# A decoder trunk on one core: the last MLP's down products with two groups in the seven-product form, and low weight parts made by adding transfers

## The chip, the cores and the metric

The kernel runs on one core of a Trainium2 chip. The metric is the device time of one execution in microseconds. Before the change the median of three runs is 2835.14 us (2832.22 to 2835.55). The execution that was profiled took 2834.88 us; the span from its first to its last profiled instruction is 2832.0 us.

## The reference, cut to what matters

Two decoder layers work on x (256 tokens by 2048 features, float32). Each layer is a token mixer, an attention over a memory of 256 rows, and a squared-ReLU MLP, each behind an RMS norm and added to x; a last RMS norm follows.

```python
def squared_relu_mlp(h, w_up, w_down):
    return jnp.square(jax.nn.relu(h @ w_up)) @ w_down      # w_up 2048 x 8192, w_down 8192 x 2048

for i in range(DEPTH):                                     # DEPTH = 2
    ...                                                    # mixer, then memory attention with x_w_o at its end
    x = x + squared_relu_mlp(rms_norm(x, g_ff[i]), f_w_up[i], f_w_down[i])
return rms_norm(x, g_final)
```

The change touches the down product of the second layer's MLP and, in the order of its steps, the output product (x_w_o) of both attentions.

## The kernel before, in words

**Float32 by three products.** TensorE multiplies in a rounded float32 format (fp32r). Each operand is split into a high part (its rounded copy) and a low part (operand minus high part), and a product is high times high, high times low and low times high. `split` (L100) makes both parts: ScalarE (ACT) casts `hi`, VectorE (DVE) subtracts `lo = src - hi`.

**Weights** come as tiles of 128x1024 float32 (512 KB, two k tiles of 128 rows by 512 columns): `wload` (L115) lets SyncE (SP) load one into `wraw` (4 buffers), and `wtile` splits it into `whi` and `wlo` (3 buffers each). A direct product with one weight tile has 12 matmuls of 512 columns: 2 k tiles, 2 halves of the tokens, 3 parts.

**The last MLP** (`mlp`, `nxt.closing`) goes in four blocks `b` of 2048 hidden features. A block first makes its hidden features with 8 calls of `gemm_feat` (32 weight tiles; here called the up stage): ACT and DVE evacuate each result, square it and split it into `hh` and `hl`. Then it multiplies with 16 k tiles of `w_down` by 4 column chunks of 512 (the down stage). Two column chunks together are a pair. Seven pairs go through `gemm_seven`: two in each of the blocks 0 to 2 and one in block 3. The last two column chunks go through `gemm_hid` and `gemm_last`.

**The seven-product form.** Take 4 k tiles as two halves, the tokens as two halves and the two column chunks. The direct product of these 2x2x2 blocks is 8 block products of 6 matmuls. With sums of the token side (`token_sums`, made once a block) and differences of the weights it is 7 block products, some of which go into two results: 42 matmuls in place of 48. The differences are `raw - raw` on DVE, 128x1024 each, and each of the 7 weight operands is then split on its own. Products are called P1 to P7 here after the steps of the new code. Before the change 4 of the 16 k tiles take this form and 12 are direct, so a pair has 42 + 144 = 186 matmuls, 19 splits and 4 differences. Two small results (`kept`) are copied out by ACT and added into x by DVE (`gather`, L617); at the end of a pair four more `gather`s read the accumulators, two as soon as the first half of the last direct products is done and two at the very end.

**Order.** The program is written against tiles; a scheduler puts the instructions of each engine into a fixed order and sets the semaphores. Each engine then works through its own list in order, and an instruction that waits holds up all behind it.

## Time and profile before

| | |
|---|---|
| median of three runs | 2835.14 us |
| profiled execution, time and span | 2834.88 us, 2832.0 us |
| TensorE (PE) busy | 2798.7 us (99%) |
| DVE, ACT, POOL busy | 1958.4, 1393.7, 200.3 us |
| last MLP, block 0: up stage, pair 1, pair 2 | about 90.4, 42.4 and 43.8 us |
| DMA | 579.55 MB, mean 205 GB/s |

Durations of matmuls in the profile overlap: one of 512 columns lasts 0.39 us, but the next starts about 0.23 us after it. How long a stage takes is read from starts, not from the sum of durations. DVE and ACT instructions that follow each other without a wait overlap by nearly 0.1 us.

### The profile page before, as it was taken

What the parts mean: (1) busy time and instruction counts of PE and PEld (TensorE: products, weight loads), DVE (VectorE), ACT (ScalarE), POOL (GpSimd) and SP (SyncE); (2) the same over time, 40 slices, a digit from 0 to 9 for tenths busy, and PEclk for the clock granted to TensorE, in tenths of its full rate; (3) what the DMA queues carried; (4) which work ended last, traced back from release to release, by engine and by line L of the source; (5) the groups of instructions that cost most, each with busy time, mean ns of one, the idle gap of its engine ahead of it and who ended that gap; (6) DMA issues with size and microseconds to landing.
All of it is one profiled execution on the core that took longest, in us unless ns stands there. A gap on an engine that the chain in (4) does not pass through costs nothing.

```text
span 2832.0 us, 39687 instructions
## 1 busy us (share of the span) xinstructions
PE 2798.7 (99%) x15172; PEld 2346.5 (83%) x15172; DVE 1958.4 (69%) x2707; ACT 1393.7 (49%) x1801; POOL 200.3 (7%) x374
## 2 busy tenths in 40 slices
PE   9999999999999999999999999999999999999998
PEld 7888888888888888888777788888888888888886
DVE  6855655578878788787567666556676767667665
ACT  5545544454544444444455445444454545445453
POOL 0100000001022222222011000000000000000000
PEclk9999999999999999999999999999999999999999
DMA  8766665657677777777879766566556576575755
GB/s 287 238 199 204 193 180 186 180 156 237 195 220 215 224 223 220 217 223 211 236 249 286 217 213 200 175 187 192 171 179 217 163 223 186 170 217 163 221 160 155
DMA packets 180847, 579.55 MB, mean 205 GB/s; under 512 B 37440, under 2 KB 39664, under 8 KB 179888
## 3 DMA queue, kind: packets, MB, share of 16 engines
q1 hardware_dynamic: 142304, 513.34, 59.0%
q0 software_dynamic: 38208, 63.62, 8.3%
q8 instruction: 118, 1.93, 0.3%
q14 instruction: 73, 0.60, 0.1%
q10 hardware_dynamic: 144, 0.07, 0.0%
HBM read 553.88 MB, written 22.94 MB: 204 GB/s over the span
## 4 chain that ended last, share of the span: by engine, by line
PE 88%; DVE 4%; DMA 4%; issue 2%; ACT 1%; POOL 0%; DVEq 0%; POOLq 0%; SPq 0%; ACTq 0%
PE acc L166 23%; PE acc L149 21%; PE acc L681 14%; PE acc L168 12%; PE acc L766 4%; PE acc L765 4%; PE acc L764 4%; DVE wlo L102 2%; DMA Kd<-kd 1%; PE ps L547 1%; PE ps L490 1%; DMA wraw<-in_f_w_down 1%; PE ps L149 1%; ACT whi L101 1%; PE ps L217 1%
## 5 line engine op out<-in xcount | busy, mean ns | idle before, releaser
L102 DVE TENSOR_TENSOR wlo<-wraw,whi 128x1024 fp32r<-128x1024 f32 x908 | 1108.5, 1222 | 660.8 <-ACT whi L101 656.8
L101 ACT CAST whi<-wraw 128x1024 fp32r<-128x1024 f32 x908 | 955.0, 1052 | 1128.6 <-PE acc L166 360.3
L166 PE MATMUL acc<-act,whi 128*128 128x512 f32 x3072 | 1082.9, 396 | 0.9 <-ACT whi L101 0.8
L168 PE MATMUL acc<-act,wlo 128*128 128x256 f32 x3072 | 865.0, 282 | 1.7 <-DVE wlo L102 1.5
L166 PEld LDWEIGHTS acc<-act,whi 128*128 128x128 f32 x3072 | 576.0, 188 | 133.9 <-ACT whi L101 1.7
L149 PE MATMUL acc<-whi,act 128*128 128x512 f32 x1984 | 623.5, 393 | 8.6 <-ACT whi L101 6.9
L168 PEld LDWEIGHTS acc<-act,wlo 128*128 128x128 f32 x3072 | 580.4, 189 | 7.0 <-DVE wlo L102 3.4
L149 PEld LDWEIGHTS acc<-whi,act 128*128 128x128 f32 x1984 | 373.0, 189 | 86.6 <-ACT whi L101 6.9
L149 PE MATMUL acc<-wlo,act 128*128 128x512 f32 x992 | 387.7, 391 | 2.0 <-DVE wlo L102 2.0
L149 PEld LDWEIGHTS acc<-wlo,act 128*128 128x128 f32 x992 | 187.0, 189 | 40.5 <-DVE wlo L102 2.9
L765 PE MATMUL acc<-wlo,hh 128*128 128x512 f32 x544 | 215.1, 395 | 0.2 <-DVE wlo L102 0.2
L764 PE MATMUL acc<-whi,hh 128*128 128x512 f32 x544 | 214.5, 394 | 0.0
L766 PE MATMUL acc<-whi,hl 128*128 128x512 f32 x544 | 214.4, 394 | 0.0
L681 PE MATMUL acc<-wlo,hh 128*128 128x512 f32 x378 | 147.6, 390 | 1.7 <-DVE wlo L102 1.6
L681 PE MATMUL acc<-whi,hh 128*128 128x512 f32 x378 | 147.6, 390 | 0.5
L681 PE MATMUL acc<-whi,hl 128*128 128x512 f32 x378 | 147.2, 389 | 0.0
L681 PE MATMUL acc<-whi,act 128*128 128x512 f32 x432 | 135.8, 389 | 0.0
L765 PEld LDWEIGHTS acc<-wlo,hh 128*128 128x128 f32 x544 | 102.2, 188 | 24.4 <-DVE wlo L102 1.5
L766 PEld LDWEIGHTS acc<-whi,hl 128*128 128x128 f32 x544 | 102.2, 188 | 22.8 <-issue 1.6
L764 PEld LDWEIGHTS acc<-whi,hh 128*128 128x128 f32 x544 | 102.2, 188 | 22.2 <-issue 0.4
L681 PEld LDWEIGHTS acc<-whi,act 128*128 128x128 f32 x432 | 80.8, 188 | 16.7 <-ACT kept L710 0.2
L681 PEld LDWEIGHTS acc<-wlo,hh 128*128 128x128 f32 x378 | 71.0, 188 | 17.9 <-DVE wlo L102 3.1
(320 smaller groups left out, 2562.5 us busy)
## 6 DMA issues: line engine op xcount, KB each, us to landing
wraw<-in_f_w_up SPq DMA_DIRECT2D x256, 512.0 KB, 4.2
wraw<-in_f_w_down SPq DMA_DIRECT2D x228, 512.0 KB, 4.3
wraw<-in_a_w_in SPq DMA_DIRECT2D x64, 512.0 KB, 4.5
wraw<-in_x_w_q SPq DMA_DIRECT2D x64, 512.0 KB, 3.7
wraw<-in_x_w_k SPq DMA_DIRECT2D x64, 512.0 KB, 3.7
wraw<-in_x_w_v SPq DMA_DIRECT2D x64, 512.0 KB, 3.7
wraw<-in_b_w_out SPq DMA_DIRECT2D x64, 512.0 KB, 4.4
wraw<-in_x_w_o SPq DMA_DIRECT2D x48, 512.0 KB, 3.9
```

Of the source, the lines that this page charges most:

```text
L101: self.nc.scalar.copy(out=hi, in_=src)
L102: self.nc.vector.tensor_tensor(out=lo, in0=src, in1=hi.bitcast(F32), op=ALU.subtract)
L149: nc.tensor.matmul(out[t], pairs[m][0][:, kt, sl], pairs[m][1][:, kk, :], start=st and m == 0, stop=en and m == 2)
L166: nc.tensor.matmul(acc[:, f, :], hi[:, kk, sl], both[:, kt].rearrange("p a s -> p (a s)"), start=st, stop=False, skip_group_check=True)
L168: nc.tensor.matmul(acc[:, f, 0:S], lo[:, kk, sl], ah[:, kt, :], start=False, stop=en, skip_group_check=True)
L217: nc.tensor.transpose(pt[:, kk, t * P:(t + 1) * P], src[:, t, c:c + P], self.ident)
L490: mm = lambda s, m, b, e: nc.tensor.matmul(sc[:, t, :], s, m, start=b, stop=e, skip_group_check=True)
L547: mm = lambda s, mv, b, e: nc.tensor.matmul(op[:, k, :], s, mv, start=b, stop=e, skip_group_check=True)
L681: mm = lambda s, m, e: nc.tensor.matmul(out, s, m, start=key not in begun, stop=e, skip_group_check=True)
L764: nc.tensor.matmul(acc[:, t, :], ah[:, kt % 4, sl], hi[:, kk, :], start=st, stop=False)
L765: nc.tensor.matmul(acc[:, t, :], ah[:, kt % 4, sl], lo[:, kk, :], start=False, stop=False)
L766: nc.tensor.matmul(acc[:, t, :], al[:, kt % 4, sl], hi[:, kk, :], start=False, stop=en)
```

## The change

`gemm_seven` becomes `gemm_pair`, which takes its steps from a list of words. In the last MLP a pair now has **two groups** in the seven-product form (8 of 16 k tiles), and each numbered step makes its product for both groups. `d0`, `d1` are direct weight tiles of column chunk 0 or 1; `l0`, `l1` are direct tiles whose parts were **made ahead**: ACT casts the high part out of `wraw` into a home in `room`, a second ACT instruction writes minus the high part into another home, and a transfer that POOL issues reads the same 512 KB of weights from memory once more and adds them to it. `room` has homes for two such tiles at a time, so the parts for the tile after the next are begun when a tile's matmuls are emitted. Two tiles are begun before the MLP. `room` also holds the token sums. It takes one of the two buffers of `act`, which the attention's output features have held until then.

The weights of the seven-product form now have 8 buffers (`ws`, 4 before), the running difference `run` is gone (differences are made in place), and the results of `gemm_feat` share the buffers of `kept`. In both attentions one group is left, but the list now starts with P1 and then P5; before it was P5, P1.

Counted in the built programs, the last MLP loses 42 matmuls (14532 to 14490 in all). On DVE 14 splits of 128x1024 fall away, 28 differences of 128x1024 and one more `token_sums` a block (four additions of 128x256 and a split) come in. ACT has 14 casts fewer and, for the 35 made tiles, 70 instructions of 128x1024 more, beside 4 casts for sums. POOL issues 35 transfers of 512 KB more.

```diff
+ONE_GROUP = "1 5 2 d1 6 d1 7 d0 4 d1 3 d0 d1 d0 d1 d0 d0".split()
+TWO_GROUPS = "1 5 2 l1 6 l1 7 l1 4 l0 3 l0 d0".split()
...
-            ws = lambda: mp.tile([P, KB * NB], F32, name="ws", bufs=4)
-            sm = lambda: mp.tile([P, 4, 2, P], F32R, name="sums", bufs=2)
-            run = lambda: mp.tile([P, KB * NB], F32, name="run", bufs=1)
-            kept = lambda i: mp.tile([P, NB], F32, name="kept", bufs=4)
+            ws = lambda: mp.tile([P, KB * NB], F32, name="ws", bufs=8)
+            kept = lambda i=None: mp.tile([P, NB], F32, name="kept", bufs=4 if nxt.closing else 2)
+            if nxt.closing:
+                room = self.act.tile([P, 8, KB * NB], F32R, name="room", tag="act")
+                homes = cycle(range(4))
...
+                low = self.low_parts(lambda: room[:, next(homes)], made)
+                for _ in range(2):
+                    low[1]()
...
-                    if nxt.closing and n == 0:
-                        sums = self.token_sums(ws(), sm, *rs)
+                    if nxt.closing and n < 2:
+                        sh, sl = (room[:, 4 + 2 * n + i].rearrange("p (s k c) -> p s k c", s=4, k=2) for i in range(2))
+                        sums.append(self.token_sums(ws(), iter((sh, sl)).__next__, *rs))
...
+        def more():
+            for w, n, kc in islice(plan, 1):
+                hi, lo = home(), home()
+                nc.scalar.copy(out=hi, in_=self.wload(w, n, kc))
+                nc.scalar.activation(out=lo, in_=hi.bitcast(F32), func=AF.Copy, scale=-1.0)
+                nc.gpsimd.dma_start(out=half(lo), in_=w[n, kc], accum_op=ALU.add)
+                ready.append((half(hi), half(lo)))
...
+        def block(key, t, i, j):
+            for q in groups:
+                into(key, lambda kk: token(KB * (2 * q + i) + kk, t), *parts(raw[q, i, j]))
+
+        def summed(key, k, i, j, minus=None):
+            for q in groups:
+                src = raw[q, i, j]
+                if minus is not None:
+                    src = raw[q, 0, minus]
+                    v.tensor_tensor(out=src, in0=raw[q, i, j], in1=src, op=ALU.subtract)
+                left = (lambda kk: [f[:, k, kk, :] for f in sums[q]]) if k < 4 else (
+                    lambda kk: token(KB * (2 * q + 1) + kk, 1))
+                into(key, left, *parts(src))
...
+            hi, lo = low[0]() if made else self.wtile(w, n0 + j, kc0 + kc)
             for t in (first, 1 - first):
+                into((t, j), lambda kk: token(KB * kc + kk, t), hi, lo)
                 yield
+            if made:
+                low[1]()
...
+        for step in order:
+            if step == "1":
+                block((1, 0), 0, 0, 0)
+            elif step == "5":
+                summed((0, 1), 0, 0, 1, 0)
+                part[5], part[1] = keep((0, 1), 0), keep((1, 0), 1)
+            elif step == "2":
+                block((0, 0), 0, 1, 0)
+            elif step == "6":
+                summed((1, 0), 1, 1, 1, 0)
+                add(0, 0, part[1])
+                part[6] = keep((1, 0), 2)
...
+            else:
+                for _ in direct(int(step[1]), int(step[1]), step[0] == "l"):
+                    pass
```

Three places in the lists of the engines follow. The first is DVE at the passage from pair 1 to pair 2 of a block (block 1 here; blocks 0 and 2 read alike). `acc` into `x` are the closing gathers of pair 1, `ws` are weights of pair 2. Before:

```order
L102 TENSOR_TENSOR wlo_21568<-run_21565,whi_21567 128x1024
L724 TENSOR_TENSOR run_21565<-ws_21563,run_21565 128x1024
L619 SCALAR_TENSOR_TENSOR x_5556<-acc_21238,r2_18986,x_5556 128x512 x2
L102 TENSOR_TENSOR wlo_21578<-ws_21557,whi_21577 128x1024
L619 SCALAR_TENSOR_TENSOR x_5556<-acc_21239,r2_18986,x_5556 128x512 x2
L102 TENSOR_TENSOR wlo_21592<-ws_21561,whi_21591 128x1024
L102 TENSOR_TENSOR wlo_21604<-wraw_21601,whi_21603 128x1024
```

And after, with the low parts of P1 (first group), P1 (second), P5 (first), P5 (second) and P2 (both) in this order:

```order
L115 TENSOR_TENSOR wlo_21603<-ws_21586,whi_21602 128x1024
L730 TENSOR_TENSOR ws_21586<-ws_21590,ws_21586 128x1024
L638 SCALAR_TENSOR_TENSOR x_5554<-acc_21263,r2_18982,x_5554 128x512 x2
L730 TENSOR_TENSOR ws_21590<-ws_21594,ws_21590 128x1024
L638 SCALAR_TENSOR_TENSOR x_5554<-acc_21264,r2_18982,x_5554 128x512 x2
L115 TENSOR_TENSOR wlo_21613<-ws_21588,whi_21612 128x1024
L115 TENSOR_TENSOR wlo_21624<-ws_21586,whi_21623 128x1024
L730 TENSOR_TENSOR ws_21588<-ws_21592,ws_21588 128x1024
L730 TENSOR_TENSOR ws_21586<-ws_21594,ws_21586 128x1024
L730 TENSOR_TENSOR ws_21592<-ws_21596,ws_21592 128x1024
L115 TENSOR_TENSOR wlo_21635<-ws_21588,whi_21634 128x1024
L115 TENSOR_TENSOR wlo_21649<-ws_21598,whi_21648 128x1024
```

Before, two low parts of the new pair stand ahead of the very last gathers; after, one does, and three differences stand between the low parts of P5's two groups.

The second place is ACT where the last MLP begins (`act` are the MLP's normed inputs on their way from PSUM, `junk` the sums of squares, `whi_19081`/`whi_19088` the high part of the third up tile). Before:

```order
L101 CAST whi_18993<-wraw_18991 128x1024
L101 CAST whi_19037<-wraw_19035 128x1024
L101 CAST whi_19081<-wraw_19079 128x1024
L179 ACTIVATE junk_19031,ss_18302<-x_5556 128x512
L179 ACTIVATE junk_19033,ss_18302<-x_5556 128x512
L101 CAST whi_19103<-wraw_19101 128x1024
L226 ACTIVATE act_18301<-ps_19013,gcol_89 128x256
```

And after:

```order
L114 CAST whi_19000<-wraw_18998 128x1024
L114 CAST whi_19044<-wraw_19042 128x1024
L682 CAST room_18983<-wraw_18984 128x1024
L682 CAST room_18983<-wraw_18989 128x1024
L683 ACTIVATE room_18983<-room_18983 128x1024 x2
L239 ACTIVATE act_18299<-ps_19020,gcol_89 128x256
L239 ACTIVATE act_18299<-ps_19029,gcol_89 128x256
L192 ACTIVATE junk_19038,ss_18300<-x_5554 128x512
L239 ACTIVATE act_18299<-ps_19020,gcol_89 128x256
L239 ACTIVATE act_18299<-ps_19029,gcol_89 128x256
L192 ACTIVATE junk_19040,ss_18300<-x_5554 128x512
L114 CAST whi_19088<-wraw_19086 128x1024
```

The third up tile's cast moved behind the four instructions into `room`, four of `act` and two of `junk`; the first of those into `room` waits until the attention's last matmul has read the buffer.

The third place is new: ACT in the middle of pair 1, where the first made tile's homes are filled again for the third (`wraw_21359`) and the second's for the fourth (`wraw_21401`). The CASTs into `room` wait for the last matmuls of the first and the second made tile.

```order
L114 CAST whi_21407<-ws_21269 128x1024
L682 CAST room_18983<-wraw_21359 128x1024
L683 ACTIVATE room_18983<-room_18983 128x1024
L750 COPY kept_21387<-acc_21263 128x512
L114 CAST whi_21418<-ws_21271 128x1024
L682 CAST room_18983<-wraw_21401 128x1024
L114 CAST whi_21450<-ws_21265 128x1024
L683 ACTIVATE room_18983<-room_18983 128x1024
```

On PE 36 matmuls stand between a made tile's last matmul and the first one that needs the low part which takes its place: a numbered step of 12, the other made tile's 12 and another step of 12.

## The prediction

> **What bounds the kernel now.** I read the busy shares and the chain of waits first, then the stages of the last MLP, then the engines' lists in time where the change acts. From the page:

> ```profile
> PE 2798.7 (99%) x15172; PEld 2346.5 (83%) x15172; DVE 1958.4 (69%) x2707; ACT 1393.7 (49%) x1801; POOL 200.3 (7%) x374
> ...
> PE 88%; DVE 4%; DMA 4%; issue 2%; ACT 1%; POOL 0%; DVEq 0%; POOLq 0%; SPq 0%; ACTq 0%
> ```

> PE sets the end: almost every matmul taken away is time, and almost every pause of PE is lost. The chain gives the pace (start, length, what, how many); the windows give pair 1 and pair 2 of block 0 and pair 1 of block 1.

> ```profile
> 2030.20 42.70 PE acc L681 x188
> 2251.30 39.51 PE acc L681 x173
> ```

> ```profile
> 2204.60:2247.00 42.40, 42.21 (x186) 34.27 (x185) 31.21 (x31) 22.31 (x25) 0.00 (x0) 1.00 0.62 198
> 2247.00:2290.80 43.80, 43.25 (x191) 35.52 (x190) 29.83 (x30) 22.51 (x24) 0.00 (x0) 1.00 0.52 156
> 2381.10:2423.30 42.20, 42.06 (x187) 34.46 (x185) 31.49 (x31) 22.49 (x25) 0.00 (x0) 1.00 0.65 199
> ```

> 42.70 / 188 is 0.227 us from one matmul to the next, at a granted clock of 1.00. So a pair's 186 matmuls take 42.2 us, and pair 1 (42.4, 42.2) runs at that pace with 0.2 us to spare for waits at most. DVE is busy 31.2 of 42.4 us there. That is the cover that the change uses up.

> **What is removed.** 42 matmuls, six in each of seven pairs: 42 x 0.227 = **9.5 us gained**. It is a gain only while low parts arrive in time.

> **DVE at pair 2.** DVE's own work for a pair was 19 splits, 4 differences and 8 small instructions. Now it is 17 splits (14 for the steps, 3 for d0 and the two last tiles), 8 differences and the same small ones. Five splits a pair went to ACT and the transfers, so the total hardly moves; but the early steps are dense. A step's product for one group is 6 matmuls, 1.36 us of PE, and wants a split and mostly a difference from DVE. The present passage from pair 1 to pair 2 shows the prices (DVE, then PE):

> ```profile
> 2243.48 1.22 DVE L102 TENSOR_TENSOR wlo<-run,whi 128x1024 fp32r<-128x1024 f32 x1 [1.50 <-ACT whi L101]
> 2244.74 1.23 DVE L724 TENSOR_TENSOR run<-ws,run 128x1024 f32<-128x1024 f32 x1
> 2245.89 1.40 DVE L619 SCALAR_TENSOR_TENSOR x<-acc,r,x 128x512 f32<-128x512 f32 x2
> 2247.56 1.23 DVE L102 TENSOR_TENSOR wlo<-ws,whi 128x1024 fp32r<-128x1024 f32 x1 [0.28 <-ACT whi L101]
> 2248.71 1.40 DVE L619 SCALAR_TENSOR_TENSOR x<-acc,r,x 128x512 f32<-128x512 f32 x2
> 2250.03 1.22 DVE L102 TENSOR_TENSOR wlo<-ws,whi 128x1024 fp32r<-128x1024 f32 x1
> ...
> 2254.09 1.22 DVE L102 TENSOR_TENSOR wlo<-wraw,whi 128x1024 fp32r<-128x1024 f32 x1
> 2255.23 1.22 DVE L734 TENSOR_TENSOR run<-ws,run 128x1024 f32<-128x1024 f32 x1
> ```

> ```profile
> 2247.64 0.39 PE L681 MATMUL acc<-whi,sums 128*128 128x512 f32 x1
> ...
> 2250.36 0.39 PE L681 MATMUL acc<-whi,hh 128*128 128x512 f32 x1
> 2251.30 0.50 PE L681 MATMUL acc<-wlo,hh 128*128 128x512 f32 x1 [0.55 <-DVE wlo L102]
> ```

> An instruction of 128x1024 costs 1.14 us when another follows (2254.09 to 2255.23), two gathers 1.32 (2248.71 to 2250.03). Pair 2 starts at 2247.64 and goes on until the matmul of 2250.36; the next one needs a low part and starts 0.94 us later, at 2251.30, in place of 0.23: PE loses 0.7 us there.

> Now put the new list on the same clock, from the gathers at 2245.89 on: two gathers to 2247.2, a difference to 2248.4, two gathers to 2249.7, then low parts of P1's second group (2250.9) and P5's first (2252.0), three differences (2255.4), low parts of P5's second group (2256.6) and of P2's two (2257.7, 2258.9). PE starts P1's first group at 2247.64 and can go no further than one matmul into its second at 2249.2; it waits to 2250.95 (1.7 us). P5's first group ends at 2253.45. Two matmuls later, at 2253.9, it waits for P5's second low part until 2256.65 (2.8 us); P2 then just finds its parts. Pauses: 4.5 us against 0.7 now, **3.8 us more in each of three blocks, 11.4 us**. After P2 comes a made tile that needs no DVE, and from there DVE is ahead again. Bounds: 0 if DVE came into the passage with those parts done (its list forbids it: the gathers wait for PE), 5 if the loads of `ws` are late too.

> **Pair 1** meets the up stage's last evacuation among its first splits, but P1's first part and two differences are done before. The same count from its list gives 0.6 us of pauses against 0.2: **1.6 us for four**.

> **The attentions** do P1 before P5, so at their second pair P5's low part stands behind the last gathers. Today, DVE and PE in layer 1:

> ```profile
> 2069.69 1.22 DVE L102 TENSOR_TENSOR wlo<-ws,whi 128x1024 fp32r<-128x1024 f32 x1 [0.40 <-ACT whi L101]
> 2070.83 1.28 DVE L577 TENSOR_TENSOR x<-acc,x 128x512 f32<-128x512 f32 x2
> 2072.03 1.21 DVE L102 TENSOR_TENSOR wlo<-ws,whi 128x1024 fp32r<-128x1024 f32 x1
> ```

> ```profile
> 2069.77 0.39 PE L681 MATMUL acc<-whi,sums 128*128 128x512 f32 x1
> ```

> With the pair's start at 2069.77, gathers from 2068.0, a difference from 2069.3, gathers from 2070.4 and P5's part from 2071.7 to 2072.9, PE, done with P1 at 2071.15, loses about 1.5 us: **3.0 us for two**.

> **The start of the last MLP.** ACT (and the PE row that starts the third up tile) today:

> ```profile
> 2112.84 1.05 ACT L101 CAST whi<-wraw 128x1024 fp32r<-128x1024 f32 x1 [3.02 <-PE acc L681]
> 2114.20 1.06 ACT L101 CAST whi<-wraw 128x1024 fp32r<-128x1024 f32 x1 [0.30 <-PE acc L681]
> 2115.78 0.63 ACT L179 ACTIVATE junk<-x 128x512 f32<-128x512 f32 x1 [0.53 <-DVE x L577]
> 2116.32 0.18 ACT L179 ACTIVATION_READ_ACCUMULATOR junk<-x 128x1 f32 x1
> ...
> 2118.10 0.83 ACT L226 ACTIVATE act<-ps,gcol 128x256 fp32r<-128x256 f32 x2
> ```

> ```profile
> 2121.25 0.47 PE L166 MATMUL acc<-act,whi 128*128 128x512 f32 x1
> ```

> The third tile's cast is done at 2115.3, six us ahead. Now four instructions of 1.03 us stand in its place, from 2114.2 (the attention's last matmul has been read) to 2118.3; four of `act` (1.6) and two of `junk` (1.5) bring the cast to 2121.4 and 2122.4, the low part to 2123.7. PE needs that from its second matmul, at 2121.5: **2.2 us lost**, once. What queues behind on ACT (the fourth tile's cast) ends at 2125.0 and its low part at 2126.2, when PE is just through with the third.

> **The adding transfers.** The trace has none. Their chain: a made tile's last matmul ends 0.39 us after its start, ACT casts (1.05) and writes minus the high part (as long, by the same shape), POOL issues. With 0.1 for wake-ups this is 2.6 us. PE has 36 matmuls, 8.2 us, plus the 0.23 of the last one before it needs the low part. So the transfer may take 5.7 us from issue to landing. The nearest rows (queue, then KB each and median us; then all transfers of `memc`, some of them issued by SP):

> ```profile
> q1 hardware_dynamic: 142304, 513.34, 59.0%
> wraw<-in_f_w_down SPq DMA_DIRECT2D x228, 512.0 KB, 4.3
> pq<-Pd POOLq DMA_DIRECT2D x16, 512.0 KB, 7.2
> memc<-in_mem_t POOLq DMA_DIRECT2D x8, 512.0 KB, 5.0
> ```

> ```profile
> DMA to landing us min/median/max: 3.0/6.6/9.7
> ```

> [...] One 512 KB holds the 16 DMA engines for 0.59 x 2832 us x 0.524 / 513.34 = 1.7 us. [...] The upper end is 9.7, the worst plain one. The stage already has the DMA engines 62% busy, and ten more transfers' worth of reading in two pairs adds to that. I take 6.3, nearer the median and most of a second read: 0.6 us late. In pair 2 the third and the fifth made tile are late by that (the fourth gains from the third's pause); in pair 1 ACT casts for a numbered step between the fourth tile's two instructions, and the third and fourth share the loss. Two pauses in each of seven pairs: 14 x 0.6 = **8.4 us**; 0 at the lower end, 14 x 4.0 = 56 at the upper.

> [...] No run here shows an adding transfer yet.

> **The sum**, on the profiled execution's 2834.88 us (0.26 below the median of the three): -9.5 + 11.4 + 1.6 + 3.0 + 2.2 + 8.4 = +17.1, **2852 us**, 0.6% slower.

> **Rivals.** *The matmuls are simply gone* (chance 0.23): DVE, busy 31 of 42 us, makes up its lead as it does now, and the transfers land within 5.7 us. Only the start's 2.2 is lost: 2834.9 - 9.5 + 2.2 = 2827.6, faster. It decides if PE's pauses at the passages stay near 0.7. For it speaks that DVE has a quarter of its time free and that PE follows a made tile with no DVE at all; against it the fixed list. *The transfers are hidden, the passages are not* (0.22): 2834.9 + 8.7 = 2843.6. For it the 5.0 row. *The transfers are slow* (0.12), 9.7 us under load: 2843.6 + 56 = 2900. For it speaks the 62% DMA share, to which pair 1 adds the loads of pair 2's eight `ws` tiles; against it that most plain ones land in half of that. My forecast holds 0.43. That the form isn't taken as described can be left out: the counts of matmuls show it.

> **Range and chances.** 2829 cuts off about half of the first rival, 2882 the last one: 2829 to 2882 holds 8 in 10. A measurement of this kernel tells apart about 0.2%, 5.7 us. Faster by more than that: 0.20, from the first rival. Within it: 0.03 from there, 0.09 of the second rival (if a passage costs 1 us less, it is below 2840.8) and 0.03 of the forecast, 0.15. Slower: 0.65.

> **What would show it.** Right: in pair 2 PE idles for `wlo` of `ws` twice, nearly 2 and 3 us, and pair 2 is longer than pair 1 by 3 us or more; PE waits for the landing of `room` before third and fifth made tiles; the third up tile of the last MLP waits for ACT. The landing time of `room` settles the rivals: under 5.7, no wait. Wrong: pairs of 41 us each, or pauses at a place not named, such as d0's load, which SP holds behind waits for `ws` buffers.

## The result, and the profile after

The changed kernel takes 2881.29 us in the median of five runs (2875.22 to 2885.58) against 2835.08 us before: 1.0163 times as long, 95% interval 1.0145 to 1.0181. The forecast was 2852 with a range to 2882, so slower was right and the size was not: 46 us were lost in place of 17. The profiled execution took 2885.58 us, 4.3 above the median, with a span of 2883.9 against 2832.0 us. One execution of the run with other orders (5160.32 us, at a clock of 0.81) and one of the kernel before (11894.22 us) took far longer than all others and are left out of every figure here. From its page, the busy shares, the chain of waits and the adding transfers (the last column is the median time from issue to landing):

```profile
PE 2814.9 (98%) x15130; PEld 2345.1 (81%) x15130; DVE 1981.5 (69%) x2741; ACT 1451.1 (50%) x1861; POOL 231.9 (8%) x409
...
PE 84%; DVE 6%; DMA 5%; ACT 2%; issue 2%; POOL 0%; DVEq 0%; ACTq 0%; SPq 0%; POOLq 0%
...
room<-in_f_w_down POOLq DMA_DIRECT2D x35, 512.0 KB, 7.9
```

The 42 matmuls are gone, yet PE is busy 16 us longer. Where the time went is seen in the windows. Before the change, cut from the first matmul of a part to the first of the next: pair 1 and pair 2 of block 0, block 3's only pair, the second attention's two pairs.

```profile
2204.63:2247.64 43.01, 42.82 (x189) 34.76 (x187) 31.57 (x32) 22.84 (x25) 0.00 (x0) 1.00 0.61 196
2247.64:2290.64 43.00, 42.45 (x187) 34.84 (x186) 29.31 (x29) 21.98 (x23) 0.00 (x0) 1.00 0.53 159
2733.33:2775.96 42.63, 42.49 (x189) 34.84 (x188) 28.61 (x29) 22.84 (x25) 0.00 (x0) 1.00 0.55 159
2024.44:2114.00 89.56, 89.56 (x414) 74.11 (x412) 64.66 (x69) 50.97 (x66) 2.13 (x4) 1.00 0.58 182
```

The same after, with pair 1 of blocks 1 and 2 as third and fourth row:

```profile
2215.14:2266.55 51.41, 45.80 (x183) 35.44 (x182) 33.46 (x34) 30.51 (x33) 4.28 (x5) 0.93 0.73 215
2266.55:2314.94 48.39, 44.13 (x181) 34.62 (x180) 32.84 (x33) 29.37 (x31) 4.32 (x5) 0.96 0.54 135
2405.39:2454.15 48.76, 44.08 (x182) 34.31 (x181) 33.34 (x34) 30.45 (x33) 4.32 (x5) 0.97 0.70 211
...
2592.75:2645.52 52.77, 45.36 (x183) 35.53 (x181) 33.34 (x34) 30.53 (x33) 4.32 (x5) 0.94 0.70 209
...
2784.17:2827.81 43.64, 42.16 (x182) 33.25 (x181) 31.93 (x33) 26.44 (x29) 2.59 (x3) 1.00 0.49 121
...
2029.88:2123.04 93.16, 91.48 (x414) 73.99 (x412) 66.30 (x71) 51.18 (x66) 2.14 (x4) 1.00 0.55 172
```

A pair with 180 matmuls would take 40.9 us at 0.227; these take 44 to 53. Pair 1, which the forecast had nearly as before, is the worst. And the granted clock (third column from the end) is below 1.00 in every pair but block 3's, which the forecast did not count on. All of it, by stage, from the starts of PE's matmuls: the seven pairs +41.4 us, the two attentions +3.3 and +3.6, the start and up stage of block 0 +1.5, and 2.1 that no edit touches (1.6 of it ahead of the first attention).

**A late transfer, and what follows it.** PE in pair 1 of block 0, at the third direct weight tile:

```profile
2238.00 0.56 PE L716 MATMUL acc<-room,hh 128*128 128x512 f32 x1 [2.25 <-DMA room<-in_f_w_down]
2238.36 0.63 PE L716 MATMUL acc<-room,hl 128*128 128x512 f32 x1
2238.78 1.05 PE L716 MATMUL acc<-room,hh 128*128 128x512 f32 x2
2239.64 0.63 PE L716 MATMUL acc<-room,hl 128*128 128x512 f32 x1
```

PE stands still for 2.4 us until the low part has landed. Then the matmuls start 0.43 us apart (2238.36, 2238.78, one more, 2239.64) in place of 0.227. The windows of the same places (4 us behind the pause; then the start of pair 1, its last 30 us and the start of pair 2, with the DMA share in the last column but one):

```profile
2238.00:2242.00 4.00, 4.00 (x11) 3.13 (x12) 1.97 (x2) 0.05 (x1) 0.00 (x0) 0.57 1.06 359
2215.00:2228.00 13.00, 12.70 (x55) 9.71 (x54) 12.97 (x14) 9.65 (x12) 0.00 (x0) 1.00 0.00 0
2235.00:2265.00 30.00, 24.70 (x93) 19.05 (x92) 12.32 (x13) 14.30 (x15) 3.43 (x4) 0.89 1.04 321
2266.00:2285.00 19.00, 15.57 (x59) 11.59 (x58) 18.04 (x18) 9.68 (x12) 0.00 (x0) 0.91 0.02 4
```

The clock was 0.57 over these 4 us: the pause of 2.4 us cost another 1.6 us behind it. And the DMA engines are idle, then full for 30 us, then idle again. SP's list shows why:

```profile
2201.24 27.75 SPq L131 DMA_DIRECT2D wraw<-in_f_w_down  x5
2229.67 3.59 SPq L704 DMA_DIRECT2D ws<-in_f_w_down  x2
2233.81 0.33 SPq L131 DMA_DIRECT2D wraw<-in_f_w_down  x1
```

The five loads of `wraw` take until 2229, since a made tile is cast only when a home is free and holds its buffer till then (the longest wait is 19.0 us); the `ws` loads of pair 2 stand behind. Then all come at once, into the stretch where the adding transfers are due.

**The passage to pair 2** went as forecast, four pauses of 1.70, 0.79, 0.72 and 1.07 us (a step over 0.227 each), 4.3 in all; but the clock fell here too, with the DMA engines at a share of 0.02 (the last window above).

```profile
2269.83 0.50 PE L716 MATMUL acc<-wlo,hh 128*128 128x512 f32 x1 [1.54 <-DVE wlo L115]
...
2273.26 0.50 PE L716 MATMUL acc<-whi,room 128*128 128x512 f32 x1 [0.63 <-ACT whi L114]
2274.21 0.49 PE L716 MATMUL acc<-whi,hh 128*128 128x512 f32 x1 [0.45 <-ACT whi L114]
2275.51 0.51 PE L716 MATMUL acc<-wlo,room 128*128 128x512 f32 x1 [0.81 <-DVE wlo L115]
```

### The profile page after: what moved, and what is told of

Its sections match the earlier page's. It is cut to its first block, busy times and chain, and to the rows that moved or that the text cites. A ratio compares the mean times of both kernels' runs of the same rounds, so it can differ in the third digit from the quotient of the medians.

```text
span 2883.9 us, 39772 instructions
## 1 busy us (share of the span) xinstructions
PE 2814.9 (98%) x15130; PEld 2345.1 (81%) x15130; DVE 1981.5 (69%) x2741; ACT 1451.1 (50%) x1861; POOL 231.9 (8%) x409
## 3 DMA queue, kind: packets, MB, share of 16 engines
q1 hardware_dynamic: 142304, 513.34, 55.1%
## 4 chain that ended last, share of the span: by engine, by line
PE 84%; DVE 6%; DMA 5%; ACT 2%; issue 2%; POOL 0%; DVEq 0%; ACTq 0%; SPq 0%; POOLq 0%
PE acc L179 23%; PE acc L162 20%; PE acc L181 12%; PE acc L716 10%; PE acc L809 4%; PE acc L808 4%; PE acc L807 4%; DMA room<-in_f_w_down 3%; DVE wlo L115 2%; ACT whi L114 1%; PE ps L503 1%; PE ps L560 1%; PE ps L162 1%; DMA wraw<-in_f_w_down 1%; DMA wraw<-in_f_w_up 1%
## 5 line engine op out<-in xcount | busy, mean ns | idle before, releaser
L115 DVE TENSOR_TENSOR wlo<-wraw,whi 128x1024 fp32r<-128x1024 f32 x845 | 1032.4, 1223 | 667.3 <-ACT whi L114 664.4
L114 ACT CAST whi<-wraw 128x1024 fp32r<-128x1024 f32 x845 | 888.2, 1052 | 1072.0 <-PE acc L179 359.8
L179 PE MATMUL acc<-act,whi 128*128 128x512 f32 x3072 | 1082.6, 396 | 1.9 <-ACT whi L114 1.9
L179 PEld LDWEIGHTS acc<-act,whi 128*128 128x128 f32 x3072 | 576.0, 187 | 134.6 <-ACT whi L114 2.4
L162 PEld LDWEIGHTS acc<-wlo,act 128*128 128x128 f32 x992 | 187.4, 189 | 41.4 <-DVE wlo L115 3.7
L808 PE MATMUL acc<-wlo,hh 128*128 128x512 f32 x544 | 215.1, 395 | 0.6 <-DVE wlo L115 0.5
L807 PE MATMUL acc<-whi,hh 128*128 128x512 f32 x544 | 214.5, 394 | 0.0
L809 PE MATMUL acc<-whi,hl 128*128 128x512 f32 x544 | 214.3, 394 | 0.0
L115 DVE TENSOR_TENSOR wlo<-ws,whi 128x1024 fp32r<-128x1024 f32 x126 | 151.5, 1219 | 66.7 <-ACT whi L114 66.7
L114 ACT CAST whi<-ws 128x1024 fp32r<-128x1024 f32 x126 | 130.7, 1049 | 86.0 <-DVE ws L730 32.1
L808 PEld LDWEIGHTS acc<-wlo,hh 128*128 128x128 f32 x544 | 102.2, 188 | 24.3 <-DVE wlo L115 1.7
L716 PE MATMUL acc<-room,hh 128*128 128x512 f32 x280 | 96.5, 418 | 19.6 <-DMA room<-in_f_w_down 19.5
L730 DVE TENSOR_TENSOR ws<-ws 128x1024 f32<-128x1024 f32 x72 | 86.7, 1219 | 0.9
## 6 DMA issues: line engine op xcount, KB each, us to landing
wraw<-in_f_w_up SPq DMA_DIRECT2D x256, 512.0 KB, 4.4
wraw<-in_f_w_down SPq DMA_DIRECT2D x200, 512.0 KB, 4.5
wraw<-in_a_w_in SPq DMA_DIRECT2D x64, 512.0 KB, 4.4
wraw<-in_x_w_q SPq DMA_DIRECT2D x64, 512.0 KB, 3.7
wraw<-in_x_w_k SPq DMA_DIRECT2D x64, 512.0 KB, 3.6
wraw<-in_x_w_v SPq DMA_DIRECT2D x64, 512.0 KB, 3.6
wraw<-in_b_w_out SPq DMA_DIRECT2D x64, 512.0 KB, 4.4
ws<-in_f_w_down SPq DMA_DIRECT2D x56, 512.0 KB, 5.9
```

What stands on the lines that cost most here:

```text
L114: self.nc.scalar.copy(out=hi, in_=src)
L115: self.nc.vector.tensor_tensor(out=lo, in0=src, in1=hi.bitcast(F32), op=ALU.subtract)
L162: nc.tensor.matmul(out[t], pairs[m][0][:, kt, sl], pairs[m][1][:, kk, :], start=st and m == 0, stop=en and m == 2)
L179: nc.tensor.matmul(acc[:, f, :], hi[:, kk, sl], both[:, kt].rearrange("p a s -> p (a s)"), start=st, stop=False, skip_group_check=True)
L716: nc.tensor.matmul(banks[key], s, m[:, kk, :], start=key not in begun, stop=m is hi and s is al, skip_group_check=True)
L730: v.tensor_tensor(out=src, in0=raw[q, i, j], in1=src, op=ALU.subtract)
```

## The experiments

Pairs are given as above, from the first matmul of one to the first of the next. A kernel's time stands beside runs of the kernel before on the same chip.

### All low parts on DVE

```diff
-TWO_GROUPS = "1 5 2 l1 6 l1 7 l1 4 l0 3 l0 d0".split()
+TWO_GROUPS = "1 5 2 d1 6 d1 7 d1 4 d0 3 d0 d0".split()
```

> The five made tiles a pair become plain tiles again (cast on ACT, subtraction on DVE, no adding transfer); all else is as in the changed kernel. DVE gets 35 splits of 1.14 us more (40 us in all, about 5.7 us a pair). Theory (late transfers and the half clock that follows their pauses cost about 33 of the 41 us by which the pairs of blocks 0 to 3 grew): pauses for room are gone; pair 1 takes 41.5 to 43.5 us (51.4, 48.8, 52.8 before), block 3's pair 42 (43.6). Pair 2 keeps the pauses at its start (4.3 us and 2 us at half clock) and may gain some from DVE, since after P2 a direct tile wants DVE too: 47 to 50 us (48.2 to 48.4). The kernel 2850 to 2862 us, about 25 faster than the changed one and still 0.5 to 1% slower than before. Rival (DVE can't take the splits: its work for a pair is 37 us of 41 and dense in the first steps): pair 1 stays at 46 or more by waits for wlo, the kernel at 2870 or more.

Measured: 2857.32 us, 1.0091 times before (1.0076 to 1.0106), 24 us less than the changed kernel. Block 0's pairs:

```profile
2213.14:2257.08 43.94, 42.38 (x182) 33.22 (x181) 39.02 (x39) 26.11 (x28) 0.00 (x0) 1.00 0.55 191
2257.08:2303.18 46.10, 42.28 (x181) 33.47 (x180) 38.98 (x38) 24.71 (x26) 0.00 (x0) 1.00 0.34 102
```

Pair 1 is 7.5 us shorter than in the changed kernel, but 0.4 longer than expected; pair 2 is 2.3 shorter, below the 47 to 50 expected. The clock is 1.00 in all pairs but one, pair 2 of block 2 (47.2 us). So the transfers cost more than they saved; but DVE is busy 39 of 44 us, PE still waits for `wlo` in both pairs, and a pair is longer than before the change.

### Half the loads of pair 2

```diff
             for q in groups:
-                fetch(q, i, j)
+                if low and n0 == 2 and q == 1:
+                    raw[1, i, j] = raw[0, i, j]
+                else:
+                    fetch(q, i, j)
```

> This kernel leaves work out: in the second pair of each of the blocks 0 to 2 the four weight tiles of the second group aren't loaded, the second group computes on the tiles of the first. So pair 2 brings 2 MB of loads in place of 4 MB, and these loads are issued during pair 1. In the changed kernel the DMA engines are idle from 2210 to 2228 us of block 0 and 100% busy from 2235 to 2265, and in that stretch the adding transfers take 8 to 9.7 us from issue to landing, while the transfers of pair 2 (with no loads of ws behind it) take 5.8 to 6.6. Theory A (the loads of the next pair, held up by their buffers, bunch in pair 1 and slow the transfers): in pair 1 the transfers land within 7 us, PE's pauses for room are under 1 us each, no stretch at half the granted clock is left in pair 1, and pair 1 takes 42 to 45 us in place of 51.4, 48.8 and 52.8. Rival (an adding transfer in pair 1 is slow of itself, or its chain on ACT and POOL is): 8 to 9.7 us as before and pair 1 at 48 to 53 us. Pair 2 isn't compared, since its differences now depend on each other.

Measured: pair 1 takes 46.3, 47.2 and 46.8 us, 4.2 less in the mean, neither the 42 to 45 of the one nor the 48 to 53 of the other. The whole, in one run, is no faster (2882.09 us): pair 2, where the differences now overwrite tiles that both groups read, got 3 to 4 us longer. The first two transfers of a pair 1, still amid the loads of the first group, take 7.6 to 9.4 us, the other three 6.3 to 8.9. What sorts them is the company. For each adding transfer of the last MLP's pairs, in this run, in the changed kernel and in the one with other orders (below), I took from the issues and landings how many other transfers were in flight on average, counted from the ends of the issuing instructions:

| others in flight (rounded) | adding transfers | issue to landing, mean us |
|---|---|---|
| 0 | 12 | 5.6 |
| 1 | 30 | 6.3 |
| 2 | 19 | 7.8 |
| 3 | 23 | 8.7 |
| 4 | 9 | 9.2 |
| 5 | 6 | 8.6 |

The bunch is a cause, then, but not all of it: with one other in flight, as in most of a pair 2, a transfer takes 6.3 us and is still late.

### Plain transfers in place of the adding ones

```diff
-                nc.gpsimd.dma_start(out=half(lo), in_=w[n, kc], accum_op=ALU.add)
+                nc.gpsimd.dma_start(out=half(lo), in_=w[n, kc].bitcast(F32R))
```

> The changed kernel with plain transfers in place of the adding ones: same instructions, same queue, same bytes written, but what was in the home isn't added, so the low parts of the made tiles are wrong. Alone in flight an adding transfer has taken 5.3 to 5.8 us (second pairs of the run with half the loads), with three others 8.7, with four 9.2. The plain 512 KB from POOL that the kernel before has took 5.0. Theory (it is the company, not the addition, that makes them late): plain ones take 5.0 to 5.3 alone and 7.5 to 8.5 among three or four others, pair 1 still over 47 us, the kernel 2866 to 2876 us, 5 to 15 faster than the changed one. [...]

Measured: 2858.89 us, 1.0085 times before (1.0069 to 1.0101), 22 less than the changed kernel. Least, median and greatest time to landing, first of the changed kernel, then of this one (all uses of `room`):

```profile
DMA to landing us min/median/max: 5.8/7.9/10.6
```

```profile
DMA to landing us min/median/max: 4.2/5.6/9.3
```

By company, plain ones take 4.6 us alone (4 of them), 4.9 with one other (10), 6.2 with two (9), 7.1 with three (4), 7.6 with four (3) and 8.5 with five (3). So the addition costs 1.0 us alone and 1.6 with two to four others, and next to nothing with five (8.6 against 8.5, from few transfers). Three others in flight cost 2.5 us for a plain transfer and 3.1 for an adding one, so company weighs more than the addition. The time came out 7 us below the 2866 to 2876 of the theory; pair 1 takes 46.8, 45.5 and 48.6 us in the slowest of the four executions, where over 47 were expected. My theory that only the company counts falls. Against the 5.7 us that there are, company alone is enough (a plain transfer with two others takes 6.2), and the addition is with one other in flight (6.3 in place of 4.9), but not alone (5.6). A late transfer also puts off the next one's issue: in the changed kernel's block 0 ACT waits 4.37 us for the matmuls of the late third tile before it fills that home again, and the next transfer is issued at 2244.85, 8.9 us after the one before it.

### Pauses alone

The kernel before, with a cast on ACT repeated 6 to 13 times ahead of every eighth weight tile of the up stages:

```diff
-            hi, lo = self.wtile(w, n, kc)
+            hi, lo = self.wtile(w, n, kc, extra=next(STALLS) if kc == 0 and n % 2 == 1 else 0)
...
+        for _ in range(extra):
+            nc.scalar.copy(out=hi, in_=raw)
         self.split(hi, lo, raw)
```

> The kernel before the change, with 6 to 13 repeated casts on ACT (each about 0.95 us, the same tile cast again) ahead of every eighth weight tile of the up stages, so that PE meets pauses of growing length, from under 1 to some 6 us, some 22 us apart, with no adding transfer near. In the changed kernel, stretches of 7 to 10 matmuls at 0.43 us in place of 0.227 stand behind pauses of 2.4, 2.6, 3.1, 3.5 and 3.9 us and behind four pauses of together 4.3 us within 6 us, and none behind 1.9 us. Theory (the pause itself brings the clock down): here too no slow stretch behind single pauses under 2 us, one behind nearly all over 3 us, 1.4 to 2.0 us lost in each, at a granted clock of about 0.5. Rival (the slow steps belong to the operands of room or to the busy DMA engines): no slow stretch here whatever the pause. [...]

Measured (STALLS goes round 6 to 13; one run, 3386.62 us): half clock without any adding transfer, behind every one of the MLPs' long pauses (4.4 to 12.0 us). One of them, with the window behind it:

```profile
2204.70 0.80 PE L170 MATMUL acc<-act,whi 128*128 128x512 f32 x1 [5.56 <-ACT whi L103]
```

```profile
2206.50:2210.00 3.50, 3.50 (x14) 2.97 (x13) 1.68 (x2) 0.00 (x0) 0.00 (x0) 0.56 0.81 238
```

The rival, that it belongs to `room` or to busy DMA engines, falls: this kernel has no `room`, and at the passage above the DMA engines were idle (a share of 0.02). But the pauses came out longer than meant and said nothing on 2 to 4 us. Hence a second run, with 2, 3, 4, 3, 5, 2, 3 and 4 casts by turns:

> As the first run with repeated casts, but with 2 to 5 of them in place of 6 to 13. There the pauses in the MLPs came out at 5.1 to 12 us, all with half clock behind them, and so said nothing about the 2 to 4 us at stake; one cast less has been about 1 us less, so 1 to 4 us are expected now. Theory (a pause of 2 us leaves the clock, one of 3.5 brings it down, between them it depends on when it falls): after pauses under 2 us no step over 0.4 us, after some of those from 2.2 to 3.3 us and after all over 3.5 us a stretch of 6 to 10 steps of 0.43. Rival (only pauses of over 4 us do it by themselves, and the 2.4 to 2.6 us in the changed kernel did it because of the shorter pauses around them): none under 4 us.

Measured in one run (2943.44 us). Four pauses of it, in PE's rows; then, for the third and the fourth, the stretch of 3.41 us in which PE fell idle and the next one (length, PE's busy time, clock, DMA):

```profile
2416.09 0.39 PE L172 MATMUL acc<-act,wlo 128*128 128x256 f32 x1 [1.54 <-DVE wlo L104]
...
2228.13 0.58 PE L172 MATMUL acc<-act,wlo 128*128 128x256 f32 x1 [1.90 <-DVE wlo L104]
...
2783.32 0.38 PE L172 MATMUL acc<-act,wlo 128*128 128x256 f32 x1 [2.26 <-DVE wlo L104]
...
2597.60 0.39 PE L172 MATMUL acc<-act,wlo 128*128 128x256 f32 x1 [2.22 <-DVE wlo L104]
```

```profile
2780.89:2784.30 3.41, 1.15 (x7) 1.00 0.42 167
2784.30:2787.71 3.41, 3.41 (x12) 0.50 0.71 205
...
2593.16:2596.57 3.41, 1.92 (x10) 1.00 0.77 303
2596.57:2599.98 3.41, 2.38 (x14) 1.00 0.45 103
```

By idle time the pauses are 1.54, 1.90, 2.26 and 2.22 us. Over the 4 us behind them the clock was 1.00, 0.59, 0.62 and 1.00: the fourth, as long as the third, left it. So length alone doesn't decide. The record of the granted clock shows more. In the traces here, up to a program's end, the clock fell to 0.50 for 3.41 us, or for two to four times that, and within a trace these pieces start on one grid of 3.41 us: in the changed kernel, where there are nine of 3.41 us, at 2238.31, 2255.38 and 2275.86 in block 0, five and six lengths apart. In the stretches of the grid just ahead of these nine PE was idle for 1.71 to 2.76 us; in the others of that kernel, its start and end aside, for at most about 1.7. In the run with short pauses the pause of 2.26 us lies in one stretch (3.41 - 1.15 = 2.26 us idle). The one of 2.22 us lies across two, with 1.49 and 1.03 us idle, and left the clock at 1.00. There the stretches at full clock that are followed by half clock have 1.6 to 3.0 us of idle time, the others at most 1.5; over all runs the two kinds overlap between 1.4 and 1.8, so the exact condition stays open.

Of the theory it stands that it depends on when a pause falls; its lower bound does not, since 1.90 us sufficed. The rival (nothing under 4 us) falls.

### Other orders of steps

ONE_GROUP begins "5 1 2" and TWO_GROUPS "1 2 5", with P2's loads ahead of P5's:

```diff
-ONE_GROUP = "1 5 2 d1 6 d1 7 d0 4 d1 3 d0 d1 d0 d1 d0 d0".split()
-TWO_GROUPS = "1 5 2 l1 6 l1 7 l1 4 l0 3 l0 d0".split()
+ONE_GROUP = "5 1 2 d1 6 d1 7 d0 4 d1 3 d0 d1 d0 d1 d0 d0".split()
+TWO_GROUPS = "1 2 5 l1 6 l1 7 l1 4 l0 3 l0 d0".split()
```

> The changed kernel with two other orders of steps: the attentions begin with P5, P1 again (as before the change), and in the last MLP P2 comes ahead of P5 (1 2 5 in place of 1 5 2, the loads in the order of their use). Theory: the attentions give back the 3.5 us each that they have lost, 7 us in two; at the passage from pair 1 to pair 2 PE meets P1's and P2's parts, which need no differences, and its pauses fall from 4.3 us (and 2 us at half clock) to 1 to 2.5 us with no half clock, 3 to 5 us a block, 9 to 15 us in three. With 7 for the attentions 2860 to 2868 us. Rival for the attentions (their loss comes from the differences made in place, or from the two step lists' buffers, not from the order): the attentions stay at 93.1 us. Rival for the passage (DVE is short of time there in total, so the pauses only move to P5): the sum of pauses and half clock in the first 60 matmuls of pair 2 stays over 5 us.

In this kernel P5's difference, made in place, overwrites what P1 of the attentions reads after it, so the attentions compute something else; the instructions are the same. Measured: 2873.24 us, 1.0150 (1.0133 to 1.0167), where 2860 to 2868 was expected. The attentions take 91.0 and 92.4 us, from one part's first matmul to the next part's, where the changed kernel has 93.1 and 93.2 and the kernel before 89.8 and 89.6: the order gives back only part. Block 0's first 60 matmuls of pair 2 take 16.4 us in place of 19.8, with 2.7 us of pauses and no half clock, a little over the 1 to 2.5 of the theory; 0.8 of it is a wait for a `kept` copy. Further on PE waited for another copy (1.1 us) and for a transfer (1.2), and pair 2 as a whole got only 1.8 us shorter.

### The attentions as before

```diff
-                self.gemm_pair((ws, kept), lambda kt, t: [f[:, kt, t * P:(t + 1) * P] for f in oT[:2]],
-                               [sums], wo, j, 0, gather, ONE_GROUP)
+                self.gemm_seven((ws, run, kept), lambda kt, t: [f[:, kt, t * P:(t + 1) * P] for f in oT[:2]],
+                                sums, wo, j, 0, gather)
```

> The changed kernel with both attentions as they were before the change (P5 ahead of P1, the running difference in a tile of its own, the old order of loads). Theory: each attention is 3.5 us shorter again (89.5 us for its two pairs in place of 93.1), the kernel about 7 us faster than the changed one, 2874. Rival (the attentions' loss is absorbed later or comes from elsewhere, as PE's delay of 5.0 us behind the first attention shrank to 3.6 later on): under 4 us in total.

Measured: the attentions take 89.9 and 89.6 us, 3.2 and 3.6 less: the theory stands, in the stage. The whole, 2877.41 us (1.0145, 1.0120 to 1.0170), is 4 us below the changed kernel; the runs of either spread over 10 us or more, so the total can't tell 4 from 7.

### Low parts on POOL

```diff
-                nc.scalar.copy(out=hi, in_=self.wload(w, n, kc))
-                nc.scalar.activation(out=lo, in_=hi.bitcast(F32), func=AF.Copy, scale=-1.0)
-                nc.gpsimd.dma_start(out=half(lo), in_=w[n, kc], accum_op=ALU.add)
+                raw = self.wload(w, n, kc)
+                nc.scalar.copy(out=hi, in_=raw)
+                nc.gpsimd.tensor_tensor(out=lo, in0=raw, in1=hi.bitcast(F32), op=ALU.subtract)
```

> The low parts of the five made tiles a pair are made by a subtraction on POOL (raw minus high part, straight from the loaded tile) in place of the ACT copy and the adding transfer; all else as in the changed kernel. No run has a POOL subtraction of 128x1024 yet. Theory (what hurts is the transfer's latency and volume): a subtraction of 2 to 4 us lands well within the 8 us that a made tile has, so no pause for room is left; ACT has 35 instructions and the DMA engines 18 MB less; pair 1 takes 41.5 to 43.5 us, pair 2 47 to 48 (its start is unchanged), the kernel 2846 to 2856 us. [...]

Measured: 2876.36 us, 1.0150 (1.0133 to 1.0167); pair 1 takes 47.2, 48.8 and 49.3 us. The groups of POOL and DVE in this kernel (busy time, mean ns of one):

```profile
L684 POOL TENSOR_TENSOR room<-wraw,room 128x1024 fp32r<-128x1024 f32 x35 | 103.6, 2961 | 607.8 <-ACT room L683 607.8
```

```profile
L115 DVE TENSOR_TENSOR wlo<-ws,whi 128x1024 fp32r<-128x1024 f32 x126 | 176.6, 1418 | 34.9 <-ACT whi L114 34.5
...
L638 DVE SCALAR_TENSOR_TENSOR x<-kept,r,x 128x512 f32<-128x512 f32 x21 | 27.3, 1298 | 1.0 <-ACT kept L750 0.9
```

A POOL subtraction is quick enough (3.0 us; the 2 to 4 expected were an estimate that no run stood behind), but DVE's subtractions of `ws` get longer, from 1219 to 1418 ns in the mean over all of them, and the 21 gathers of `kept` from 748 to 1298. In pair 1 PE's longest pause, 4.0 us, is a wait for DVE's low part of P7's second group: in block 0 a gather ahead of it (2231.61) took 2.6 us and the subtraction itself (2235.28) 3.4, while POOL worked from 2229.35 to 2233.68 and from 2234.50 to 2237.56. The theory falls: DVE, the engine that was to be relieved, is slowed.

### Two made tiles a pair

```diff
-TWO_GROUPS = "1 5 2 l1 6 l1 7 l1 4 l0 3 l0 d0".split()
+TWO_GROUPS = "1 5 2 l1 6 l1 7 d1 4 d0 3 d0 d0".split()
```

> The changed kernel with two made tiles a pair in place of five (the first two direct tiles, l1 after P2 and l1 after P6); the other three are cast and subtracted like any tile. Both homes are then filled while the pair before still runs, 30 us and more ahead, and only 14 adding transfers are left. Theory (what costs is that a transfer of 6 to 10 us must land within 36 matmuls): no pause for room is left, whatever a transfer takes; pair 1 takes 42.5 to 44 us, pair 2 keeps its start (4.3 us, perhaps with half clock) and takes 46 to 47.5, the kernel 2850 to 2856 us, a little below the kernel with all low parts on DVE (2857), since DVE has two splits fewer in the dense part. Rival (the transfers hurt by their volume, not by when they land): pair 1 stays over 46 us.

Measured: 2843.19 us, 1.0031 (1.0020 to 1.0041), 38 us less than the changed kernel by one word in three places, and 7 less than the least that was expected; both pairs are shorter than expected too. Block 0's pairs, and the transfers:

```profile
2210.51:2252.50 41.99, 41.67 (x182) 33.32 (x181) 36.94 (x37) 27.72 (x30) 1.71 (x2) 1.00 0.65 224
2252.50:2297.89 45.39, 41.95 (x181) 33.57 (x180) 36.51 (x36) 26.47 (x28) 1.69 (x2) 1.00 0.45 127
```

```profile
DMA to landing us min/median/max: 5.8/7.6/10.2
```

The transfers take as long as ever (5.8 to 10.2 us) and nobody waits for one: they are issued 30 us ahead. Not how long a transfer takes was the trouble, but that it was begun 36 matmuls before its use. (There are also fewer of them, 14 in place of 35, but these take no less time.) Against the kernel with all low parts on DVE the 14 made tiles are worth about 15 us. Pair 1 is a full microsecond shorter than before the change. What is left is the passage, 4.5 us of pauses in pair 2 (6 steps), the attentions, and the start.

### Four edits together, then the end made ahead

```diff
-TWO_GROUPS = "1 5 2 l1 6 l1 7 l1 4 l0 3 l0 d0".split()
+TWO_GROUPS = "1 2 5 l1 6 l1 7 d1 4 d0 3 d0 d0".split()
...
-                for _ in range(2):
-                    low[1]()
+                for d in (12, 16):
+                    self.at(d, low[1])
...
-        for i, j in ((0, 0), (0, 1), (1, 1), (1, 0)):
+        for i, j in ((0, 0), (1, 0), (0, 1), (1, 1)):
```

and `gemm_seven` in the attentions, as above.

> Four edits together: two made tiles a pair; in the last MLP P2 ahead of P5 (1 2 5), with the loads in the order of use; both attentions as before the change; the first two made tiles begun 12 and 16 weight tiles into the up stage in place of ahead of it. Theory, term by term against the kernel with all low parts on DVE (2857): attentions -7, start of the MLP 0 to -1.5, passage -2 to -3 in each of three blocks, dense first steps -0.5 to -1 in seven pairs: 2835 to 2842 us, still not faster than before (2833), because 1.4 us gained a pair are eaten by what is left of DVE's waits. Rival (DVE isn't the limit once the order is mended): pairs of 41.5 us or less and 2826 to 2830 us, faster than before.

Measured: 2840.35 us, 1.0017 (1.0006 to 1.0027). The attentions gave back what they should, and the pause at the start is gone (the up stage still took as long, for the reason in the last point of this document). "1 2 5" brought nothing against the kernel with two made tiles: pair 1 took 42.9 us in place of 42.0, pair 2 44.9 in place of 45.4. The forecast of 2835 to 2842 held near its upper end, though the term of the passage did not: pair 2 is 1.2 us shorter than with all low parts on DVE, where 2 to 3 were expected. The rival (pairs of 41.5) falls.

The passage was then taken from another side. At the end of a pair two direct tiles are open at once and hold two of three `wlo` buffers, so DVE can't begin the second part of P1, whatever the order of steps. In the next kernel the last tile of column chunk 1 is a made one, the order is 1 5 2 again, and the attentions and the late start of the first two tiles stay as in the one before:

```diff
-TWO_GROUPS = "1 5 2 l1 6 l1 7 l1 4 l0 3 l0 d0".split()
+TWO_GROUPS = "1 5 2 l1 6 d1 7 d1 4 d0 3 d0 d0".split()
...
             if made:
-                low[1]()
+                self.at(made, low[1])
...
-        ends = [direct(0, 1), direct(1, 0)]
+        ends = [direct(0, 1), direct(1, 0, 3 * bool(low))]
```

> Two groups with two made tiles a pair: the first direct tile after P2, and the very last one, of column chunk 1. Each home then has a whole pair to be refilled, and the refill is begun four and three weight tiles after it came free, off the dense steps. With no split for the last tile two of the three wlo buffers are free before the pair ends, so DVE and ACT make both of P1's parts and a difference before the gathers. The attentions are as before the change, the first two made tiles begun 12 and 16 weight tiles into the up stage. Theory (what is left in the kernel with two made tiles is the passage, 3.5 us a block over a pair without waits, and the attentions): PE's pauses in the first third of pair 2 fall from 4.5 to 1 us or less; pairs of 41.5 to 42.5 us, 296 us for the seven in place of 300 before the change, and the attentions as before: 2826 to 2831 us, 0.15 to 0.3% faster than the kernel before. Rival (DVE, with 37 us of work in a pair of 41, has no room for the steps after P2): pauses move to P6 and P7, pairs of 43 or more, 2835 or more.

Measured: 2830.16 us in the median of eleven runs, 0.9987 times before (0.9978 to 0.9996). This is the one version that is faster than the kernel before, by 0.13%, about 4 us, with an interval that ends just short of 1. Pair 1 and pair 2 of block 0, and DVE at the passage:

```profile
2203.32:2245.98 42.66, 42.19 (x182) 33.31 (x181) 39.26 (x39) 26.86 (x29) 0.85 (x1) 1.00 0.56 197
2245.98:2288.09 42.11, 41.60 (x181) 33.50 (x180) 35.03 (x35) 26.82 (x28) 1.70 (x2) 1.00 0.55 148
```

```profile
2239.11 1.23 DVE L115 TENSOR_TENSOR wlo<-ws,whi 128x1024 fp32r<-128x1024 f32 x1 [1.50 <-ACT whi L114]
2240.37 2.48 DVE L731 TENSOR_TENSOR ws<-ws 128x1024 f32<-128x1024 f32 x2
2242.77 1.22 DVE L115 TENSOR_TENSOR wlo<-ws,whi 128x1024 fp32r<-128x1024 f32 x1
2243.91 1.40 DVE L639 SCALAR_TENSOR_TENSOR x<-acc,r,x 128x512 f32<-128x512 f32 x2
```

Both of P1's parts are done at 2244.0, 2 us before the pair starts; in the changed kernel the second came 3.2 us after it. Pauses in the first third of pair 2 are 0.8 us (before the change 0.8). The seven pairs take 296.9 us against 300.0 before the change. That is 3 us in two single executions, and no more can be read from them: the stretch between the attentions, in which no edit differs among the runs of the changed kernel, takes 1357.8 to 1365.0 us in their profiles. The 4 us rest on the medians.

## Why the prediction was wrong

Its steps, with what the profiled execution has in their place (pauses are steps between matmul starts, less 0.227):

| term | forecast | measured |
|---|---|---|
| 42 matmuls fewer | -9.5 | -9.5 (42 x 0.227) |
| passage to pair 2, three blocks | +11.4 | +10.7 of pauses (4.3 a block, less 0.7 before) |
| start of pair 1 | +1.6 | +0.7 of pauses (0.48 a pair, less 0.30 before) |
| attentions | +3.0 | +6.9 |
| start of the last MLP | +2.2 | +1.5 |
| late adding transfers | +8.4 | +22.2 (6.9, 5.6, 8.2 and 1.5 in blocks 0 to 3) |
| half clock after pauses | not seen | +12.3 (4.7, 2.8, 4.8 in blocks 0 to 2) |
| slower restarts behind pauses (0.1 us each) and small steps | not seen | about 5 |
| no edit's | | +2.1 |

**Right:** PE sets the end and follows the lists of DVE; the passage was counted out from the list to 0.2 us (1.7 for P1's second part, as measured; 2.8 for P5's, 2.6 measured in three pieces). The budget of 5.7 us for a transfer was right as well: in pair 2 one issued at 2286.24 and landed at 2292.50, 6.26 later, made PE wait 0.56. (Two small misses cancel in it: 37 matmuls stand between, not 36, and the chain up to the issue took 2.9 us, not 2.6.) The third and the fifth made tile are the late ones, as forecast for pair 2; pair 1 has the same two. **Right in kind, too small:** "I take 6.3" for the transfer. It counts most of a second read, which no run shows; beside plain transfers the addition took 1.0 us more alone, 1.4 with one other in flight and 1.6 with two to four. 6.3 us is what one takes with one other in flight, which is pair 2. There block 0 has two pauses of 0.6, as forecast, block 1 one of 0.7 and block 2 three of 0.2 to 0.4. In pair 1 of blocks 0 to 2 all but two of fifteen take 7.9 to 9.7, since loads bunch there and the addition adds 1.6 in company. The step that failed is that one number for all pairs: the term came to 22.2 us in place of 8.4, and pair 1, not pair 2, became the longer one. The prediction had the upper end, 9.7, and had named the loads of pair 2 as what speaks for it, but gave it 12%, as a case for every pair alike; it held in three. SP's list, with the `ws` loads behind a `wraw` load that waits for a home, had the bunch in it, and wasn't put on the clock as DVE's was.

**Missing:** the clock, a term of 12.3 us that the sum did not have. The last MLP of the kernel before doesn't show it; PE pauses for no more than 0.7 us there. Elsewhere that trace has it once: the clock was 0.50 from 1543.90 to 1547.31, behind a stretch of 3.41 us in which PE was busy for 1.71. The runs with pauses alone show it behind idle time of PE without any adding transfer (1.90 and 2.26 us in the one with short pauses). It added about 1.6 us to each of the five waits of 2.4 us and more for a transfer.

**Luck:** the measured time is still inside the range, just below its upper end of 2882, but that end was not drawn for such a sum. The time got there by 13.8 us more of late transfers, the 12.3 us of half clock and 3.9 us more in the attentions.

**A misread cut:** the prediction cut pair 1 of block 0 at 2247.0, while its own PE row has pair 2 start at 2247.64. Before the change the two pairs take 43.0 us each, not 42.4 and 43.8, so pair 1 had not 0.2 but 0.4 to 0.8 us of pauses and restarts in it. The term for the start of pair 1 took its 0.2 from there; with 0.4 it would have been 0.8 us, near the 0.7 measured.

**The attentions** cost twice the forecast and in another place. The wait for P5's part at the second pair is small (0.4 us). PE waits later in that pair, 0.6, 0.35 and 0.7 us, in layer 0 from 636.7 on. DVE's and then ACT's rows there:

```profile
636.70 0.69 DVE L778 TENSOR_TENSOR kept<-kept 128x512 f32<-128x512 f32 x1 [0.47 <-ACT kept L750]
637.31 1.22 DVE L730 TENSOR_TENSOR ws<-ws 128x1024 f32<-128x1024 f32 x1
```

```profile
636.08 0.59 ACT L750 COPY kept<-acc 128x512 f32<-128x512 f32 x1 [1.65 <-PE acc L716]
638.61 1.05 ACT L114 CAST whi<-ws 128x1024 fp32r<-128x1024 f32 x1 [1.95 <-DVE ws L730]
639.57 1.04 ACT L114 CAST whi<-wraw 128x1024 fp32r<-128x1024 f32 x1
```

The addition of two kept results has moved from behind P3 up to P7 and waits there for ACT's copy; the difference for P4 stands behind it on DVE, and P4's cast on ACT behind that, with the next tile's cast. The diff shows the moved addition; the prediction did not cost it. That it is this addition is read from the rows; no run moved it alone. Putting back all of the old form returns 6.8 us; P5 ahead of P1 alone returned 2.9.

**The start** was the ACT queue, as forecast: PE's second matmul of the third up tile waits for its low part.

```profile
2132.06 0.39 PE L181 MATMUL acc<-act,wlo 128*128 128x256 f32 x1 [0.76 <-DVE wlo L115]
```

With the two made tiles begun later the pause is gone. **Pair 1's start** cost less than forecast: its one pause, 0.48 us, is a wait for P2's first low part, where the kernel before has 0.30 a little earlier.

## What to carry to other kernels

A transfer on a critical path is sized by its worst company, not by a median (here 5.6 us alone, 9.2 with four others in flight), and it was cheaper to begin it earlier than to make it shorter: fewer made tiles, each with a whole pair to land in, were worth 38 us, plain transfers 22. Before work is taken off a busy engine, look at what its buffers let it do ahead: one open tile less at the end of a pair removed a pinch that the other order of steps did not. A pause of PE can cost more than its length: here one of 2.4 us cost another 1.6 us behind it, at a clock of 0.57.
